# Which engine issues two kinds of DMA, and how many buffers hold a state-space unit's inputs

## The chip, the cores and the metric

The kernel runs on one core of a Trainium2 chip. A core has five engines that run side by side, each through its own instructions in order: TensorE (PE, matrix products; its weight loads are shown as PEld), VectorE (DVE), ScalarE (ACT), GpSimd (POOL) and SyncE (SP, which only issues DMAs). SP, ACT and POOL can issue DMAs; the bytes are carried by 16 DMA engines beside them. An instruction that waits for another engine or for a DMA waits in its place, and whatever stands behind it on the same engine waits with it.

The metric is the device time of one execution in microseconds; lower is better.

## The reference

One layer of a hybrid encoder, for one sequence of 2048 frames and 1024 channels, in float32. One normalised input `h` goes through one projection; its columns feed a diagonal state-space mixer (32 groups of 16 channels, 64 complex states each) and chunked attention (8 heads of 64, each chunk of 64 frames looks at itself and 8 chunks to its left). Both outputs are normalised, joined and projected, and a gated feed-forward network follows.

```python
h = rmsnorm(x, norm_mix_g[l])
proj = h @ w_in[l]
u_ssm, q, k, v = ...            # columns of proj
y_ssm = s5_mixer(u_ssm, ...)    # states = scan(lam_bar, B u); y = Re(C states) + D u; GELU, GLU
y_att = chunked_attention(q, k, v, attn_rel_bias[l])
mixed = concatenate([rmsnorm(y_ssm, ...), rmsnorm(y_att, ...)])
x = x + mixed @ w_out[l]
h2 = rmsnorm(x, norm_ffn_g[l])
x = x + (silu(h2 @ w_gate[l]) * (h2 @ w_up[l])) @ w_down[l]
return rmsnorm(x, norm_final_g)
```

## The kernel before

The work runs in stages: a prologue that builds the state-space matrices together with the projection of `u` (to about 150 us), the attention stage (about 150 to 720 us), the join and output projection (to about 1000 us), the gate and up products and then the down product. Matrix products are made from three float32r products of high and low halves (`mm3`, or the same three lines written out), which is why most operands exist as a "hi" and a "lo" tile.

The planner of the kernel's language places tiles in buffers, adds the waits, and orders the instructions of each engine: it keeps to the order of the code as a priority, and takes a later instruction first where an earlier one is not ready by its own estimate. TensorE's instructions are pinned to the order of the code (`Ordered`, `k.ta`, `k.te`); those of ACT, DVE, POOL and SP in the attention stage mostly are not.

**The attention stage** (`att_phase`) is a list of 128 steps: 4 blocks of 512 frames (`sb`), 4 pairs of heads (`pr`), 2 heads of a pair (`hh`), 4 groups of 128 queries (`qp`). A step issues, in this order, the scores of step s (`scores`: products `sc`, then on DVE the bias and the row extreme, line 846, then on ACT the exponential, line 849); the transposes of step s - 2 (`transp`: products `pt` into the only bank of that name, copied by ACT as `pth`, line 864, and by DVE as the low half `ptl`, line 865); the products with V (`pv_head`, `pv_scale`); and then parts of "units" that fill TensorE's time:

* `qk_unit(sb, pr)`: projects the queries (c = 0) and the keys (c = 1) of a pair of heads. The result of the queries lies in one bank `pf`, the first head in partitions 0 to 63, the second in 64 to 127. For each head, ACT writes the high half `q2h` into its own 64 partitions (line 769), DVE the low half `q2l` (line 770), and two DMAs, lines 771 and 772, copy each half into the other 64 partitions of the same tile. The second head's ACT instruction comes behind the first head's DVE instruction, since both read the one bank.
* `v_unit`, and `hT_unit`, which loads and normalises the next block's input (`xt`, `hi`, `lo`; lines 714 to 729).
* `ssm_unit(b)`, b = 0 to 7: four groups of 16 state-space channels each. It loads the frames `U` (8 DMAs), the input matrices `Bst`, the Toeplitz matrices `Tm` (8 DMAs) and the state-output matrices `Vm`, all issued by SP (line 567). After 8 empty turns the first product, `U` with `Bst`, goes through ACT (line 591) into the tile `X`. POOL scans `X` over time (lines 605 to 617) and copies the states with four DMAs to `XG` (line 639). After 9 more empty turns come the second products: `U` with `Tm` plus `XG` with `Vm`, copied by ACT (line 649) into `Y`, which shares its single buffer with `X`. Eight DMAs (line 652), issued by SP, store `Y` to memory as `S["y"]`. A unit fills 15 of the 128 steps, and the next follows.

`U`, `Bst`, `Tm` and `Vm` have one buffer each. The loads of the next unit's `U`, `Tm` and `Vm` can thus be issued only when the products of the unit before have read them. Unit 0's loads alone are pinned in the order of the code. In the units POOL is the engine `eng`.

The join (`mix_phase`) reads `S["y"]` back as `yr` (line 1030) in four loads for two blocks of frames, each load waiting for the stores of two units; GELU on ACT follows (line 1034), then the products of the gate (`gh`, `gl`).

POOL writes the descriptors of its own DMAs into a space of SBUF that the program reserves when it is made; its size was the default, 16384 bytes of each partition.

Of the kernel before, what the change touches and what calls it, by code (L numbers as in the profile page):

```python
# [16 lines left out]
P = 128  # L17
# [3 lines left out]
NG, CH, NS = 32, 16, 64  # L21
NPR = NG // 2
L = 8
NC = SEQ // L
GB, GP = 4, 2
# [81 lines left out]
def f32(ap):  # L107
    return ap.bitcast(F32)
# [48 lines left out]
def mm3(te, out, whi, wlo, xhi, xlo, first, last, **kw):  # L157
    te.matmul(out, whi, xhi, start=first, stop=False, **kw)
    te.matmul(out, whi, xlo, start=False, stop=False, **kw)
    te.matmul(out, wlo, xhi, start=False, stop=last, **kw)  # L160
# [399 lines left out]
def ssm_unit(k, p, psum, S, b, eng):  # L560

    nc = k.nc
    F = GB * CH
    U = k.t(p, "U", [P, GB, NC])

    def load(out, in_):
        ins = nc.sync.dma_start(out, in_)
        if b == 0:
            k.tc.keep_in_program_order(ins)

    for j in range(L):
        load(U[j * CH : (j + 1) * CH], S["u"][b * F : (b + 1) * F, j, :].rearrange("(g c) t -> c g t", c=CH))
    gs = slice(GB * b, GB * b + GB)
    bst = k.t(p, "Bst", [P, GB, P])
    load(bst[:].rearrange("p g m -> p (g m)"), S["bst"][b // 2][:, (b % 2) * GB * P : (b % 2 + 1) * GB * P])
    tm = k.t(p, "Tm", [P, GB, P])
    for i in range(L):
        load(tm[i * CH : (i + 1) * CH], S["kt"].rearrange("c g a m -> c g (a m)")[:, gs, P - CH * i : 2 * P - CH * i])
    vm = k.t(p, "Vm", [P, GB, P])
    load(vm[:], S["v"].rearrange("q g c n m -> (c n) (q g) m")[:, gs, CH:])  # L580
    for _ in range(YL):
        yield

    X = k.t(p, "X", [P, 2, GP, NC])
    for q in range(GP):
        ps = k.t(psum, "pj", [P, 2, NC], bufs=2)
        for g2 in range(2):
            k.ta.matmul(ps[:, g2, :], bst[:, 2 * q + g2, :], U[:, 2 * q + g2, :], start=True, stop=True)
        for g2 in range(2):
            for c in range(2):  # L590
                nc.scalar.copy(X[g2 * NS : (g2 + 1) * NS, c, q, :], ps[c * NS : (c + 1) * NS, g2, :])  # L591
        yield

    a8 = S["a8"]
    qs = slice(GP * b, GP * b + GP)
    Xk = X[:].rearrange("p r q (k s) -> p r q k s", s=8)
    Xe = Xk[:, :, :, :, 7].rearrange("p r q (a b) -> p r q a b", b=8)

    def step(dst, src, e, n):

        ar = a8[:, 0, qs, (0, 7, 15)[e]].unsqueeze(1).to_broadcast([P, 2, GP]).unsqueeze(3).to_broadcast([P, 2, GP, n])
        aw = S["sw"][:, e, :, qs].unsqueeze(3).to_broadcast([P, 2, GP, n])
        t = k.t(p, "st1", [P, 2, GP, NC // 8])
        t2 = k.t(p, "st2", [P, 2, GP, NC // 8])
        eng.tensor_tensor(t[:, :, :, :n], src, ar, op=ALU.mult)  # L605
        eng.tensor_tensor(t2[:, :, :, :n], src[:, ::-1], aw, op=ALU.mult)
        eng.tensor_tensor(dst, dst, t[:, :, :, :n], op=ALU.add)
        eng.tensor_tensor(dst, dst, t2[:, :, :, :n], op=ALU.add)

    def carry(dst, end, i0, n):  # L610

        for c in range(2):
            for e in range(2):
                t = k.t(p, "fx", [P, GP, NC // 8, 7])[:, :, :n]
                pw = a8[:, c if e == 0 else 1 - c, qs, i0 : i0 + 7].unsqueeze(2).to_broadcast([P, GP, n, 7])
                eng.tensor_tensor(t, end[:, e].unsqueeze(3).to_broadcast([P, GP, n, 7]), pw, op=ALU.mult)
                eng.tensor_tensor(dst[:, c], dst[:, c], t, op=ALU.subtract if e == 1 and c == 0 else ALU.add)
            yield

    for s in range(1, 8):  # L620
        step(Xk[:, :, :, :, s], Xk[:, :, :, :, s - 1], 0, NC // 8)
        yield
    for b_ in range(1, 8):
        step(Xe[:, :, :, :, b_], Xe[:, :, :, :, b_ - 1], 1, 4)
        yield
    for a in range(1, 4):
        step(Xe[:, :, :, a : a + 1, 7], Xe[:, :, :, a - 1 : a, 7], 2, 1)
        yield
    yield from carry(Xe[:, :, :, 1:, :7], Xe[:, :, :, :3, 7], 8, 3)
    yield from carry(Xk[:, :, :, 1:, :7], Xk[:, :, :, : NC // 8 - 1, 7], 0, NC // 8 - 1)  # L630

    if b == 0:
        k.XG = k.t(p, "XG", [P, GB, NC])
        nc.gpsimd.memset(k.XG[:, :, 0:1], 0.0)
    XG = k.XG
    XGv = XG[:].rearrange("p (q g) c -> p q g c", g=2)
    for g2 in range(2):
        for c in range(2):
            eng.dma_start(XGv[c * NS : (c + 1) * NS, :, g2, 1:], X[g2 * NS : (g2 + 1) * NS, c, :, : NC - 1])
    for _ in range(YX):  # L640
        yield
    Y = k.t(p, "X", [P, GB, NC])
    for q in range(GP):
        ps = k.t(psum, "pj", [P, 2, NC], bufs=2)
        for g2 in range(2):
            g = 2 * q + g2
            k.ta.matmul(ps[:, g2, :], tm[:, g, :], U[:, g, :], start=True, stop=False)
            k.ta.matmul(ps[:, g2, :], vm[:, g, :], XG[:, g, :], start=False, stop=True)
        nc.scalar.copy(Y[:, 2 * q : 2 * q + 2, :], ps[:])
        if q == GP - 1:  # L650
            for j in range(L):
                nc.sync.dma_start(S["y"][b * F : (b + 1) * F, j, :].rearrange("(g c) t -> c g t", c=CH), Y[j * CH : (j + 1) * CH])
        yield


# [25 lines left out]
def att_phase(k, ident, S):  # L681
    tc, nc, io = k.tc, k.nc, k.io
    with ExitStack() as cx:
# [16 lines left out]
        def keep_w(n):  # L700
            if n in keep:
                (k.Q if n in (0, 4) else nc.sync).dma_start(S["ws"][n], f32(keep.pop(n)[:]))
# [33 lines left out]
        def qk_unit(sb, pr):  # L736
            ws = [load_w(sb, n) for n in (pr, 4 + pr)]
            yield
            hi, lo = hT[sb]
            if (sb, pr) == (0, 0):  # L740
                ts = [[k.t(aw, f"{n}{q}x", [P, SB], F32R) for n, q in (("hi", hh), ("lo", hh), (("hi", "lo")[hh], 2))] for hh in range(2)]
            else:
                ts = [(k.t(aa, "q2h", [P, SB], F32R, bufs=3), k.t(aa, "q2l", [P, SB], F32R, bufs=3), k.t(aa, "k2", [P, 2 * SB], F32R, bufs=3)) for _ in range(2)]
            qk[sb, pr] = ts
            if sb > 0:
                for hh in range(2):
                    nc.sync.dma_start(f32(ts[hh][2][:, :SB]), S["k"][(sb - 1) % 2, 2 * pr + hh])
            both = (sb, pr) == (0, 0)
            pss = []
            for c in range(2):  # L750
                if c == 0 or not both:
                    cc = range(2) if both else (c,)
                    pss += [k.t(pfs, "pf", [P, 512]) for _ in cc]
                    for q in range(KT):
                        cs = slice(q * P, (q + 1) * P)
                        for m in cc:
                            wh, wl = ws[m]
                            mm3(k.ta, pss[m][:], wh[:, cs], wl[:, cs], hi[q][:], lo[q][:], q == 0, q == KT - 1)
                            if q == 2:
                                keep_w(4 * m + pr)  # L760
                        if q < KT - 1:
                            yield
                ps = pss[c]
                for hh in range(2):
                    q2h, q2l, k2 = ts[hh]
                    a = slice(hh * 64, hh * 64 + 64)
                    o = slice(64 - hh * 64, 128 - hh * 64)
                    if c == 0:
                        nc.scalar.activation(q2h[a, :], ps[a, :], AF.Copy, scale=-0.125)
                        nc.vector.scalar_tensor_tensor(q2l[a, :], ps[a, :], -0.125, f32(q2h[a, :]), op0=ALU.mult, op1=ALU.subtract)  # L770
                        nc.sync.dma_start(f32(q2h[o, :]), f32(q2h[a, :]))
                        nc.sync.dma_start(f32(q2l[o, :]), f32(q2l[a, :]))
                    else:
                        nc.scalar.copy(k2[a, -SB:], ps[a, :])
                        nc.vector.tensor_tensor(k2[o, -SB:], ps[a, :], f32(k2[a, -SB:]), op=ALU.subtract)
                        if sb < NSB - 1:
                            nc.sync.dma_start(S["k"][sb % 2, 2 * pr + hh], f32(k2[:, -SB:]))
                yield
# [926 lines left out]
```

## Time and profile before

| | |
|---|---|
| time, median of 3 runs | 2311.45 us (2308.72 to 2311.48) |
| the profiled execution: its own time | 2304.9 us |
| the profiled execution: span from the first to the last instruction | 2303.1 us |
| mean granted TensorE clock in it | 0.975 |
| DMA issues of U, in KB each | 64 of 64 KB, by SP |
| DMA issues of Tm and of Vm | 64 of 32 KB and 8 of 256 KB, by SP |
| DMA issues of y | 64 of 64 KB, by SP |
| moves of q2h and of q2l | 30 of 128 KB each, and 2 each of the first unit in other tiles, by SP |
| DMA issues of XG | 32 of 127.5 KB, by POOL |

The views used below are: the page's list of busy times; busy time by stretches of the span; the waits of an engine (who waited, `<-`, for whom: us in total, times, longest us); the timeline of one engine (start us, length us, instruction, count, and in brackets the idle time before it with what ended it); and the list of the instructions that touch one tile or come from one line, with the shortest, the median and the longest duration in ns. `L567` is line 567 of the kernel. A name such as `pj<-U,Bst` is a tile and what it is computed from. A DMA row gives the time of its issue on the engine that issues it; the landing is given apart. A busy time counts no DMA issue of SP or ACT and no wait.

### The profile page before, as it was taken

The numbers are of one execution on the slowest core, as the hardware profiler recorded it, in microseconds if no ns is written. First come the engines' busy times: TensorE is split into PE (matmuls) and PEld (weight loads), VectorE is DVE, ScalarE is ACT, GpSimd is POOL, SyncE is SP. The second block draws the span as 40 slices with busy tenths as digits, with TensorE's granted clock in tenths as the row PEclk, the third lists the DMA queues.
The fourth block names the chain that finished last, engine by engine and source line by source line (L and its number), as shares of the span: only waits on it lengthen the run. The fifth ranks groups of instructions, "written<-read, shape, count | busy, mean of one in ns | idle before, by whom it ended". The sixth has DMA issues, their size and how long they took to land.

```text
span 2303.1 us, 30454 instructions
## 1 busy us (share of the span) xinstructions
PE 2183.8 (95%) x10568; PEld 1834.1 (80%) x10568; DVE 1487.8 (65%) x2286; ACT 1001.3 (43%) x1675; POOL 1061.0 (46%) x1245
## 2 busy tenths in 40 slices
PE   8978799999997899989999999999999999999997
PEld 6667688898986788778888887888888878888886
DVE  7845555656555756676775669766645376578676
ACT  6335555555557542343333335333333343344332
POOL 3416655455660433265555554555555314445442
PEclk9989999999998999999999999999999999999998
DMA  8788766766653534754554556555433287465552
GB/s 295 260 286 265 235 210 204 207 190 193 192 137 114 178 118 163 249 165 143 167 193 157 205 190 254 195 193 167 158 96 110 76 326 265 165 228 183 201 182 74
DMA packets 216370, 437.00 MB, mean 190 GB/s; under 512 B 27352, under 2 KB 58120, under 8 KB 209112
## 3 DMA queue, kind: packets, MB, share of 16 engines
q1 hardware_dynamic: 211352, 420.89, 55.0%
q0 software_dynamic: 4864, 14.17, 1.9%
q8 instruction: 83, 1.36, 0.2%
q14 instruction: 71, 0.58, 0.1%
HBM read 294.98 MB, written 132.15 MB: 185 GB/s over the span
## 4 chain that ended last, share of the span: by engine, by line
PE 59%; DVE 3%; DMA 1%; ACT 1%; issue 1%; POOL 1%; SPq 0%; DVEq 0%; ACTq 0%; POOLq 0%
PE X L74 20%; PE ps L74 18%; PE Y L74 10%; PE big L74 6%; PE W L74 5%; DVE acc L1575 1%; DMA lo<-hc 0%; DMA x<-xt 0%; DVE xt L1117 0%; DVE lo L166 0%; DVE hd L166 0%; POOL c L166 0%; ACT hi L165 0%; POOL sa L1125 0%; DMA gl<-x 0%
## 5 line engine op out<-in xcount | busy, mean ns | idle before, releaser
L74 PE MATMUL X<-hi,c 128*128 128x512 f32 x1408 | 452.2, 392 | 7.6 <-ACT u L1391 3.5
L74 PE MATMUL ps<-hd,hd 128*128 128x512 f32 (+1 forms) x1968 | 431.7, 381 | 3.9 <-DVE hd L166 3.7
L74 PEld LDWEIGHTS ps<-hd,hd 128*128 128x128 f32 x1968 | 358.8, 190 | 75.5 <-DVE hd L166 5.1
L166 POOL TENSOR_TENSOR c<-S,c 128x512 fp32r<-128x512 f32 x176 | 253.1, 1440 | 260.7 <-ACT c L165 258.8
L74 PEld LDWEIGHTS X<-hi,c 128*128 128x128 f32 x1408 | 265.8, 189 | 65.2 <-ACT u L1391 5.1
L74 PE MATMUL X<-lo,c 128*128 128x512 f32 x704 | 275.3, 391 | 0.0
L166 POOL TENSOR_TENSOR hd<-hd 128x1536 fp32r<-128x1536 f32 (+1 forms) x46 | 159.1, 3463 | 232.0 <-ACT hd L165 218.8
L166 POOL TENSOR_TENSOR c<-raw,c 128x512 fp32r<-128x512 f32 x132 | 189.0, 1432 | 137.5 <-ACT c L165 109.1
L165 ACT CAST hd<-hd 128x1536 fp32r<-128x1536 f32 (+1 forms) x106 | 147.4, 1393 | 219.4 <-DMA hd<-hq 134.5
L74 PE MATMUL Y<-hi,c 128*128 128x512 f32 x704 | 225.5, 391 | 4.8 <-DVE u L1395 4.8
L1521 DVE TENSOR_TENSOR acc<-acc,ps 128x512 f32<-128x512 f32 x196 | 129.2, 681 | 79.5 <-PE ps L74 79.1
L74 PE MATMUL big<-m,woh 128*128 128x512 f32 x512 | 165.4, 404 | 0.6 <-DVE m L166 0.4
L165 ACT CAST c<-S 128x512 fp32r<-128x512 f32 x176 | 109.5, 622 | 116.5 <-PE Y L74 59.1
L74 PE MATMUL pf<-hi,w 128*128 128x512 f32 x416 | 150.9, 415 | 9.4 <-ACT hi L729 5.8
L74 PEld LDWEIGHTS Y<-hi,c 128*128 128x128 f32 x704 | 132.6, 188 | 33.9 <-DVE u L1395 6.3
L74 PEld LDWEIGHTS X<-lo,c 128*128 128x128 f32 x704 | 133.0, 189 | 27.7
L1391 ACT COPY u<-X 128x512 f32<-128x512 f32 x132 | 77.1, 585 | 177.5 <-PE X L74 177.5
L846 DVE CUSTOM_DVE_ANT_0 s<-sc,nb 128x640 f32<-128x640 f32 (+4 forms) x128 | 94.4, 737 | 89.4 <-PE sc L74 85.9
L605 POOL TENSOR_TENSOR st<-X,a 128x128 f32<-128x128 f32 (+2 forms) x136 | 47.4, 349 | 220.0 <-ACT X L591 157.4
L165 ACT CAST c<-raw 128x512 fp32r<-128x512 f32 x132 | 82.1, 622 | 143.1 <-PE Y L74 80.3
L166 DVE TENSOR_TENSOR hd<-hd 128x1536 fp32r<-128x1536 f32 (+1 forms) x60 | 119.3, 1990 | 31.2 <-ACT hd L165 30.5
L74 PE MATMUL Y<-lo,c 128*128 128x512 f32 x352 | 137.2, 390 | 0.0
(462 smaller groups left out, 4644.2 us busy)
## 6 DMA issues: line engine op xcount, KB each, us to landing
w<-wss SPq DMA_DIRECT2D x36, 1024.0 KB, 5.5
hq<-g SPq DMA_DIRECT2D x140, 256.0 KB, 2.1
hd<-hq SPq DMA_DIRECT2D x42, 768.0 KB, 4.5
hd<-wc SPq DMA_DIRECT2D x42, 768.0 KB, 6.0
raw<-in_w_gate SPq DMA_DIRECT2D x44, 512.0 KB, 3.7
raw<-in_w_up SPq DMA_DIRECT2D x44, 512.0 KB, 4.1
wc<-px SPq DMA_DIRECT2D x66, 256.0 KB, 3.2
wss<-w SPq DMA_DIRECT2D x12, 1024.0 KB, 5.6
```

Of the source, the lines that this page charges most:

```text
L74: return self.tc.keep_in_program_order(self.tc.nc.tensor.matmul(*a, **b))
L165: (hi_eng or nc.scalar).copy(hi, raw)
L166: (lo_eng or nc.gpsimd).tensor_tensor(lo, raw, f32(hi), op=ALU.subtract)
L605: eng.tensor_tensor(t[:, :, :, :n], src, ar, op=ALU.mult)
L846: nc.vector.tensor_tensor_reduce(s[:, :nk].rearrange("p (a b) -> p a b", a=nch), ps[:, :nch, :half], hd.nb[:, nk - 1 :: -1].rearrange("p ( ...
L1391: nc.scalar.copy(u[:], ps[:])
L1521: V.tensor_tensor(a, a, ps[:], op=ALU.add)
L1575: nc.vector.scalar_tensor_tensor(v, v, k.go[:, i : i + 1], self.rs[:, : self.n], op0=ALU.mult, op1=ALU.mult)
```

## The change

Five edits. The unit's `U`, `Tm` and `Vm` get two buffers each, which is 8 KB more of each partition. The eight stores of `Y` are issued by the unit's own engine, POOL. The moves of the query halves are issued by ACT. The reserved space for POOL's descriptors is halved to 8192 bytes.

```diff
@@ ssm_unit
-    U = k.t(p, "U", [P, GB, NC])
+    U = k.t(p, "U", [P, GB, NC], bufs=2)
...
-    tm = k.t(p, "Tm", [P, GB, P])
+    tm = k.t(p, "Tm", [P, GB, P], bufs=2)
...
-    vm = k.t(p, "Vm", [P, GB, P])
+    vm = k.t(p, "Vm", [P, GB, P], bufs=2)
...
             for j in range(L):
-                nc.sync.dma_start(S["y"][b * F : (b + 1) * F, j, :].rearrange("(g c) t -> c g t", c=CH), Y[j * CH : (j + 1) * CH])
+                eng.dma_start(S["y"][b * F : (b + 1) * F, j, :].rearrange("(g c) t -> c g t", c=CH), Y[j * CH : (j + 1) * CH])
@@ qk_unit
-                        nc.sync.dma_start(f32(q2h[o, :]), f32(q2h[a, :]))
-                        nc.sync.dma_start(f32(q2l[o, :]), f32(q2l[a, :]))
+                        nc.scalar.dma_start(f32(q2h[o, :]), f32(q2h[a, :]))
+                        nc.scalar.dma_start(f32(q2l[o, :]), f32(q2l[a, :]))
@@ kernel
-    nc = bacc.Bacc("TRN2", target_bir_lowering=False, num_devices=1)
+    nc = bacc.Bacc("TRN2", target_bir_lowering=False, num_devices=1, dynamic_dma_scratch_size=8192)
```

`Bst` and the tile `X` of `X` and `Y` keep one buffer. No arithmetic changes.

## The prediction, made before the changed kernel was run

> **What bounds the kernel now.** I began with the page: its span, and the busy time of each engine.
>
> ```profile
> span 2303.1 us, 30454 instructions
> PE 2183.8 (95%) x10568; PEld 1834.1 (80%) x10568; DVE 1487.8 (65%) x2286; ACT 1001.3 (43%) x1675; POOL 1061.0 (46%) x1245
> ```
>
> TensorE is busy 95% of the span, so an edit is worth what it takes from, or adds to, TensorE's idle time. All edited lines run in the attention stage. The view by stretches (us, then busy time of PE, PEld, DVE, ACT and POOL with instruction counts, granted clock, DMA share, GB/s) shows how tight that stage is:
>
> ```profile
> 175.00:700.00 525.00, 487.57 (x2954) 434.89 (x2952) 303.51 (x573) 291.20 (x614) 292.69 (x704) 0.98 0.68 205
> 550.00:600.00 50.00, 50.00 (x327) 46.24 (x326) 27.42 (x50) 27.89 (x56) 19.14 (x49) 1.00 0.63 184
> 600.00:650.00 50.00, 47.28 (x271) 42.17 (x270) 25.02 (x44) 27.12 (x54) 19.90 (x49) 0.97 0.61 172
> ```
>
> TensorE idles 37 us of these 525. DVE, ACT and POOL are busy a little over half: there is room on them, but it lies in pieces. What TensorE waits for there, in the view of waits of three stretches (150 to 240, 240 to 400, 560 to 690 us; total, times, longest):
>
> ```profile
> PE pj L74 <- DMA Tm<-kts: 1.1, 1, 1.1
> ```
> ```profile
> PE pf L74 <- ACT hi L729: 5.8, 2, 3.5
> PE pj L74 <- DMA U<-u: 1.6, 1, 1.6
> PE pj L74 <- DMA Tm<-kts: 0.6, 1, 0.6
> ```
> ```profile
> PE pj L74 <- DMA U<-u: 2.7, 1, 2.7
> ```
>
> Four state-space units (of 0 to 7) start late because their loads are late: 1.1 + 1.6 + 0.6 + 2.7 = 6.0 us. The two named Tm stand before the first product (U with Bst), which reads no Tm; I read them as the frames U too. Why the loads are late is read from SyncE's timeline around unit 7, and TensorE's beside it (start, length, instruction, idle time before it and its releaser):
>
> ```profile
> 630.28 0.32 SPq L567 DMA_DIRECT2D U<-u  x1
> ```
> ```profile
> 633.40 3.86 SPq L652 DMA_DIRECT2D y<-X  x8
> ```
> ```profile
> 637.77 3.27 SPq L567 DMA_DIRECT2D U<-u  x7
> ```
> ```profile
> 642.88 2.70 PE L74 MATMUL pj<-U,Bst 128*128 128x256 f32 x8 [2.72 <-DMA U<-u]
> ```
>
> The first frame load can be issued only when unit 6 has freed U; then come unit 6's eight stores, and only then the seven other loads. The engines that carry the bytes are not the cause: the order on SyncE and the single buffer are.
>
> **The change, part by part.** *Second buffers.* With two U, unit 7's frames need no longer wait for unit 6. Will their issue move ahead? The planner does move a load that is free: Bst of unit 2 was issued 29 us before the same unit's first frames, though both stand together in the code.
>
> ```profile
> 263.08 0.38 SPq L567 DMA_DIRECT2D Bst<-bsts  x1
> ```
> ```profile
> 292.14 0.33 SPq L567 DMA_DIRECT2D U<-u  x1
> ```
>
> The longest wait is 2.7 us; 29 us ahead removes it, so I take all of the 6.0 us. The bounds are 0 and 6.0. In the stretch 600 to 650, which holds the 2.7 us wait, the clock is 0.97 against 1.00 in the one before: 0.03 x 50 = 1.5 us, which I add (bounds 0 and 1.5). What is late next is the transposes (below).
>
> *Moves of queries on ACT.* Thirty and thirty moves leave SyncE's queue for ACT's:
>
> ```profile
> L771 SPq DMA_DIRECT2D q2h<-q2h x30: 461/467/605, 171.2 to 676.7; - x30
> L772 SPq DMA_DIRECT2D q2l<-q2l x30: 461/467/1404, 172.0 to 677.6; - x30
> ```
> ```profile
> SPq L771 <- ACT q2h L769: 29.1, 14, 6.1
> SPq L772 <- DVE q2l L770: 7.6, 23, 1.1
> ```
>
> On SyncE this takes 60 x 0.467 = 28 us and 36.7 us of waiting ahead of other loads; nothing but the frames above has TensorE waiting there, so the relief itself is priced at 0. On ACT, which issues no DMA before, an issue is bounded by SyncE's 0.461 and by 1.29 us (the first unit, below); I take 0.467, the same transfer. The q2h move needs only ACT's own result. The q2l move adds a real wait: it needs DVE's low part, on average 7.6/23 = 0.33 us after the q2h issue, and behind it in ACT's order stand exponentials and the copies of the transposes, on which TensorE soon waits. A unit has two halves. ACT already idles between them:
>
> ```profile
> ACT q2h L769 <- DVE q2l L770: 6.8, 9, 0.8
> ```
>
> That idle (6.8/9 = 0.76 us) holds the first issue. In strict order the others push ACT by 0.47 + 0.47 + 0.33 + 0.47 = 1.74 us. If the planner puts other work into the waits, about one issue (0.47) stays. Does it reach TensorE? The last tight place, in the timelines of ACT, DVE and PE, and the first one on PE:
>
> ```profile
> 633.11 0.69 ACT L864 CAST pth<-pt 128x640 fp32r<-128x640 f32 x1
> ```
> ```profile
> 633.84 0.82 DVE L865 TENSOR_TENSOR ptl<-pt,pth 128x640 fp32r<-128x640 f32 x1 [0.26 <-ACT pth L864]
> ```
> ```profile
> 634.74 0.63 PE L77 MATMUL pt<-ident,s 128*128 128x128 f32 x4
> ```
> ```profile
> 204.00 0.87 PE L77 MATMUL pt<-ident,s 128*128 128x128 f32 x3 [1.81 <-DVE ptl L865]
> ```
>
> There is one transpose bank. ACT copies it, DVE ends at 634.66, and TensorE refills it 0.08 us later: a later ACT is a later TensorE. I count five of the fifteen units with under 0.2 us of room behind the moves (near 204, 275, 345, 490 and 635); in the others the next transposes come 0.7 us or more after DVE. So 5 x 0.47 = +2.3 us. The bounds are 0 (all absorbed) and 5 x 1.74 = 8.7.
>
> The four moves of the very first unit also go to ACT, just ahead of the Toeplitz and projection copies:
>
> ```profile
> 128.73 1.29 SPq L772 DMA_DIRECT2D lo0x<-lo0x  x1
> ```
> ```profile
> 127.39 3.92 ACT L413 COPY kt<-pp 16x512 f32<-16x512 f32 x8
> ...
> 140.88 0.92 ACT L304 COPY bst<-pp 128x256 f32<-128x256 f32 x3 [3.87 <-DMA bsts<-bst]
> ```
>
> ACT there feeds POOL's bsts stores, whose landing ACT awaits at 140.88, so a push goes through. Two of four issues fit idle places; the other two cost between 0 and 2 x 1.29 = 2.6; I take 2 x 0.5 = +1.0.
>
> *Stores of y by POOL.* 64 issues, bounded by SyncE's (3.86/8 = 0.48) and POOL's own moves of XG:
>
> ```profile
> L639 POOL DMA_DIRECT2D XG<-X x32: 587/621/666, 212.3 to 685.4; - x32
> ...
> DMA to landing us min/median/max: 2.3/4.7/8.7
> ```
> ```profile
> DMA to landing us min/median/max: 2.0/2.2/3.9
> ```
>
> (The second landing row is of the present y stores.) I take 0.621: 5.0 us for a unit's eight, 40 us in all. Their cover is POOL's idle time between units: the stores wait for ACT's last copy of Y, and POOL's next work is the next scan, which needs ACT's new X. At the unit change I quote from ACT:
>
> ```profile
> 359.52 0.59 ACT L649 COPY X<-pj 128x512 f32<-128x512 f32 x1 [1.10 <-PE pj L74]
> ```
> ```profile
> 370.44 1.90 ACT L591 COPY X<-pj 64x256 f32<-64x256 f32 x5 [2.15 <-issue]
> ```
>
> From 360.11 to 370.44 are 10.3 us; 5.0 are used, so 0 on the path. Y and the next X share one buffer, though: without that cover the new X waits (a rival). Only the last unit's stores have a reader at once, the read-back yr:
>
> ```profile
> 695.27 3.63 SPq L652 DMA_DIRECT2D y<-X  x8
> 702.19 0.34 SPq L899 DMA_DIRECT2D ya_s<-ya  x1
> 702.77 0.53 SPq L1030 DMA_DIRECT2D yr<-y  x1
> ```
> ```profile
> 708.88 3.64 ACT L1034 ACTIVATE ys<-yr 128x2048 f32<-128x2048 f32 x1
> ```
> ```profile
> 713.61 0.79 PE L74 MATMUL pf<-gh,wgh 128*128 128x512 f32 x1 [6.76 <-ACT gh L165]
> ```
> ```profile
> yr<-y SPq DMA_DIRECT2D x8, 512.0 KB, 5.5
> ```
>
> From 695.3, POOL issues until 700.3, landing at 702.5 to 705.0. Today yr is issued at 702.77 behind another store and lands about 5.5 later, at 708.3, 0.6 before GELU begins. From the middle, 703.7, it lands at 709.2: +0.3 us (bounds 0 and 1.6).
>
> *The smaller descriptor space.* The smaller space for POOL's DMAs pays for the buffers. No row shows POOL waiting for it; I take 0.
>
> **Sum.** -6.0 - 1.5 + 2.3 + 1.0 + 0.3 = -3.9 us. The profiled execution took 2304.9 (its span and 1.8 around it), 6.6 under the median of 2311.45; I apply the difference to the median: **2307.5 us**.
>
> **The rivals.** (a) *More comes early.* SyncE, rid of waits, also issues the next block's input tiles sooner, and the 5.8 us wait on hi goes: -9.7, 2301.7. Against it: those tiles stand behind stores of k, which stay. (b) *ACT takes the gain.* Strict order: -7.5 + 8.7 + 2.2 + 0.3 = +3.7, 2315.2. For it: the single transpose bank; against it: a planner that fills waits. (c) *The change doesn't do what it says.* The loads stay late behind other waits on SyncE, and only costs are left: +3.6, 2315.1. The Trainium skill's "DMA: Bandwidth & Descriptors", section "Issuing engines are not separate DMA queues", says all issuers share the same 16 DMA engines and another issuer saves only issue time, usually small: by it (c) is the outcome. The order of unit 7's rows speaks against it. (d) *Slower: the stores hold X.* POOL's last store of a unit is issued 5.0 us after Y; if it lands over 4.7 us later (the median of POOL's XG, so this is the deciding point), the new X, ACT behind it, the scan and its product move. At 8.7, XG's maximum, it is 4.0 us at a unit change; for half of seven changes +14, together +10, 2321.6. For it: the shared buffer; against: stores to memory land in 2.2 us now. The Trainium skill's "SBUF - State Buffer", section "SBUF: two separate sides", warns that a DVE operation holding the shared port starves POOL's descriptor writing; POOL's 587 to 666 ns for 32 issues beside a busy DVE show none of it.
>
> **How the numbers follow.** About 0.2% (4.6 us) is what a measurement of this kernel can tell from no change, so faster is under 2306.8, slower over 2316.1. Forecast case 0.46 (its own range 2303 to 2311: 0.28 faster, 0.18 same); (a) 0.13 faster; (b) 0.17 (0.13 same, 0.04 slower); (c) 0.09 (0.06 same, 0.03 slower); (d) 0.15 (0.01 same, 0.14 slower). Sums: 0.41, 0.38, 0.21. The range 2300 to 2320 takes in (a), (b), (c) and the lighter half of (d).
>
> **What would show it.** Frames issued well before their unit's product and no TensorE wait on U or Tm: the first term. Clock 1.00 at 600 to 650: the second. Move issues on ACT near 0.47 us, and TensorE's wait on DVE ptl grown by 2 to 3 us: the third; by 8: (b). Eight stores on POOL in 5 us, the X copies not waiting on them: if they do, (d). I am wrong if the planner reorders ACT or DVE elsewhere in the stage, or the stall before 141 us changes by several us.

## The result, and the profile after

The changed kernel takes **2342.09 us** (median of 5 runs, 2337.61 to 2345.67) against 2311.48 for the kernel before in the same runs: 30.6 us more, a ratio of 1.0127 with a 95% interval from 1.0109 to 1.0144. The forecast was 2307.5, its range ended at 2320.

The page of the changed kernel begins:

```profile
span 2340.1 us, 30413 instructions
PE 2194.6 (94%) x10568; PEld 1838.8 (79%) x10568; DVE 1493.4 (64%) x2286; ACT 1002.6 (43%) x1675; POOL 1088.4 (47%) x1309
```

TensorE runs the same 10568 products in the same order, so the two traces can be laid side by side product by product. Up to 124 us they agree within 1 us. By the 500th product (about 138 us) the new one is 9.1 us behind, at the 1500th 15.0, at the 2000th 28.3, at the 3500th (704.6 us) 34.4; after that it gains and loses 1 to 2 us and ends 37.0 behind. Nearly all was lost before the end of the attention stage. (The two profiled executions lie 37.0 us apart, the medians 30.6; so what is read from these two traces adds up to some 6 us more than the change in the median.) The view by stretches for the same 3200 products, from the first `pp<-vg,bbg` on, before and after (length, busy PE, PEld, DVE, ACT, POOL, clock, DMA share, GB/s):

```profile
124.28:702.10 577.82, 527.00 (x3204) 470.16 (x3202) 324.49 (x617) 315.22 (x674) 297.10 (x713) 0.97 0.69 212
```
```profile
125.14:737.70 612.56, 538.47 (x3203) 476.92 (x3201) 323.92 (x617) 316.52 (x674) 329.61 (x777) 0.95 0.66 201
```

The stretch has grown by 34.7 us. TensorE idles 23.3 us more (74.1 against 50.8), and is busy 11.5 us longer with the same products, at a clock of 0.95 for 0.97. DVE and ACT have no more work than before: it is a matter of what waits for what. POOL's 32 us more are the 64 stores.

What was hoped for came. TensorE waits for no frame any more; unit 7's frames are all issued 70 us ahead of their product (timelines of SP and PE):

```profile
595.16 2.04 SPq L567 DMA_DIRECT2D U<-u  x4
601.68 1.87 SPq L567 DMA_DIRECT2D U<-u  x4
```
```profile
673.73 1.89 PE L74 MATMUL pj<-U,Bst 128*128 128x256 f32 x8
```

In the side-by-side view the first products of units 1, 2, 3 and 7 gain 1.30, 1.76, 0.80 and 2.88 us. What was paid stands in other waits (waits of TensorE, 140 to 740 us, before and after):

```profile
PE pt L77 <- DVE ptl L865: 13.5, 10, 2.6
...
PE pj L74 <- ACT X L591: 0.2, 1, 0.2
PE pj L74 <- DVE ptl L865: 0.2, 1, 0.2
```
```profile
PE pt L77 <- DVE ptl L865: 23.2, 12, 3.0
...
PE pj L74 <- DVE ptl L865: 7.4, 9, 1.4
PE pj L74 <- ACT X L591: 6.8, 2, 3.5
```

The waits for the low half `ptl` grew by 16.9 us, and those for the copies `X` of a unit's first product by 6.6. Two timelines of the changed kernel show one place of each kind. At 451 us DVE stands for a tile `xt`, and the copy `ptl` stands behind it, so TensorE waits for the transpose bank (2.40 us):

```profile
450.40 0.75 DVE L728 SCALAR_TENSOR_TENSOR xt<-xt,g_mix,rsn 128x512 f32<-128x512 f32 x1 [4.78 <-DMA xt<-in_xt]
451.07 0.82 DVE L865 TENSOR_TENSOR ptl<-pt,pth 128x640 fp32r<-128x640 f32 x1
```
```profile
451.94 0.77 PE L77 MATMUL pt<-ident,s 128*128 128x128 f32 x5 [2.40 <-DVE ptl L865]
```

That DVE waits for `xt` is only one of the ways in which `ptl` comes late: over the stage DVE waits no longer for `xt` than before (10.3 us against 10.8). At most of the other places a bias step (line 846) or the low half of another tile stands in front of `ptl`.

At 391 us ACT stands 3.61 us for an exponential whose row extreme is not there. The eight copies of unit 3's first product, which ended at 389.69, stand behind it:

```profile
391.24 0.83 ACT L849 ACTIVATE s<-s,mn 128x640 f32<-128x640 f32 x1 [3.61 <-DVE mn L846]
391.97 0.19 ACT L849 ACTIVATION_READ_ACCUMULATOR s<-s,mn 128x1 f32 x1
392.06 3.01 ACT L591 COPY X<-pj 64x256 f32<-64x256 f32 x8
```

In the kernel before the copies of this unit began at 370.44, ahead of that exponential (the prediction quotes the row). The order in which the planner put DVE's and ACT's instructions is different, although no arithmetic is.

### The profile page after: what moved, and what is told of

The parts are those of the page before. It is cut to its first block, busy times and chain, and to the rows that moved or that the text cites. A ratio compares the mean times of both kernels' runs of the same rounds, so it can differ in the third digit from the quotient of the medians.

```text
span 2340.1 us, 30413 instructions
## 1 busy us (share of the span) xinstructions
PE 2194.6 (94%) x10568; PEld 1838.8 (79%) x10568; DVE 1493.4 (64%) x2286; ACT 1002.6 (43%) x1675; POOL 1088.4 (47%) x1309
## 4 chain that ended last, share of the span: by engine, by line
PE 57%; DVE 4%; DMA 2%; issue 1%; ACT 1%; POOL 0%; SPq 0%; DVEq 0%; ACTq 0%; POOLq 0%
PE X L74 19%; PE ps L74 18%; PE Y L74 10%; PE big L74 5%; PE W L74 5%; DMA lo<-hc 1%; DVE lo L166 1%; DVE acc L1575 1%; DMA x<-xt 0%; DVE xt L1117 0%; DVE hd L166 0%; POOL sa L1125 0%; DVE u L1395 0%; DVE m L166 0%; DMA hd<-hq 0%
## 5 line engine op out<-in xcount | busy, mean ns | idle before, releaser
L166 DVE TENSOR_TENSOR hd<-hd 128x1536 fp32r<-128x1536 f32 (+1 forms) x60 | 124.5, 2076 | 32.6 <-ACT hd L165 32.3
L865 DVE TENSOR_TENSOR ptl<-pt,pth 128x640 fp32r<-128x640 f32 (+3 forms) x152 | 98.3, 647 | 50.7 <-ACT pth L864 49.3
```

Of the source, the lines that this page charges most:

```text
L166: (lo_eng or nc.gpsimd).tensor_tensor(lo, raw, f32(hi), op=ALU.subtract)
L865: nc.vector.tensor_tensor(ptl[:, a:b, qp, :], pt[:, a:b, :], f32(pth[:, a:b, qp, :]), op=ALU.subtract)
```

## The experiments

Each kernel is compared with the kernel before in runs on the same chip.

| kernel | median us | before us | ratio, 95% interval |
|---|---|---|---|
| the change | 2342.09 | 2311.48 | 1.0127 (1.0109 to 1.0144) |
| moves_only | 2341.38 | 2309.98 | 1.0136 (1.0116 to 1.0156) |
| first_moves_only | 2318.03 | 2309.98 | 1.0031 (1.0012 to 1.0049) |
| bufs_stores | 2317.08 | 2309.98 | 1.0029 (1.0019 to 1.0039) |
| bufs_only | 2321.33 | 2309.98 | 1.0047 (1.0031 to 1.0063) |
| change_first_on_SP | 2333.82 | 2307.87 | 1.0114 (1.0099 to 1.0129) |
| moves_held | 2319.67 | 2307.87 | 1.0047 (1.0030 to 1.0064) |
| change_held | 2323.03 | 2307.87 | 1.0053 (1.0036 to 1.0071) |
| bufs_stores_held | 2328.28 | 2307.87 | 1.0084 (1.0067 to 1.0101) |
| bufs_stores_held_SP | 2305.51 | 2307.87 | 0.9985 (0.9971 to 0.9999) |
| stores_held_SP | 2305.00 | 2307.87 | 0.9981 (0.9968 to 0.9995) |
| moves_but_first_held_SP | 2309.29 | 2307.87 | 1.0004 (0.9990 to 1.0018) |
| scratch_only | 2307.14 | 2307.87 | 0.9999 (0.9986 to 1.0012) |

**The parts by themselves.** moves_only is the kernel before with this edit alone:

```diff
-                        nc.sync.dma_start(f32(q2h[o, :]), f32(q2h[a, :]))
-                        nc.sync.dma_start(f32(q2l[o, :]), f32(q2l[a, :]))
+                        nc.scalar.dma_start(f32(q2h[o, :]), f32(q2h[a, :]))
+                        nc.scalar.dma_start(f32(q2l[o, :]), f32(q2l[a, :]))
```

> The kernel before with the third part alone: the 64 moves are issued by ACT. Theory A (the moves cost all): the whole loss and no gain on the frames, 2342 + 6 = about 2348, within 2340 and 2355. Theory B (early loads alter the order, moves cost in the prologue alone): 2311.5 + 9 = about 2320.

It costs 31.4 us, as much as the whole change. Theory A had 2348 for it, by adding back the 6 us of the frames; they are not to be had that simply, as the next two show. bufs_stores is the change with the moves back on SP, bufs_only has the second buffers and the smaller descriptor space alone.

```diff
# bufs_stores: the change, but
-                        nc.scalar.dma_start(f32(q2h[o, :]), f32(q2h[a, :]))
-                        nc.scalar.dma_start(f32(q2l[o, :]), f32(q2l[a, :]))
+                        nc.sync.dma_start(f32(q2h[o, :]), f32(q2h[a, :]))
+                        nc.sync.dma_start(f32(q2l[o, :]), f32(q2l[a, :]))
# bufs_only: besides this
-                eng.dma_start(S["y"][b * F : (b + 1) * F, j, :].rearrange("(g c) t -> c g t", c=CH), Y[j * CH : (j + 1) * CH])
+                nc.sync.dma_start(S["y"][b * F : (b + 1) * F, j, :].rearrange("(g c) t -> c g t", c=CH), Y[j * CH : (j + 1) * CH])
```

> The change without its third part: second buffers, stores of y on POOL and the smaller descriptor space stay, the 64 moves of query halves go back to SP. Theory A, the moves on ACT cost all that was lost: the first units' frames still come early (-6.0), the prologue's delay of about 9 us goes, and the stage loses nothing: 2311.5 - 6 = about 2305, within 2302 and 2309. Theory B, early loads alter the order on ACT and DVE and the moves only cost in the prologue: 2342 - 9 = about 2333. Theory C, the stores on POOL hold the shared buffer: also near 2333, with X copies of ACT that wait for landings of y.

> The second buffers with the smaller descriptor space that makes room for them; stores and moves on SP. Theory A: the frames still stand behind the stores of y and the moves in the queue of SP, so a part of the 6.0 us at most comes: 2306 to 2312. Theory B: about 2333 as for bufs_stores. If this is 2305 and bufs_stores too, the stores on POOL bring nothing.

Both are slower than the kernel before, by 7.1 and 11.4 us, and neither theory had that: A expected 2305 and at most 2312, B 2333. The runs of bufs_only lie far apart (2311 to 2330), and its profiled run is the lowest of them, so its trace isn't read for the loss, and what bufs_only lost stays open. In bufs_stores the frames gain the same 1.30, 1.76, 0.80 and 2.88 us, and the copies of `X` stand behind an exponential again:

```profile
377.79 0.83 ACT L849 ACTIVATE s<-s,mn 128x640 f32<-128x640 f32 x1 [2.73 <-DVE mn L846]
378.52 0.19 ACT L849 ACTIVATION_READ_ACCUMULATOR s<-s,mn 128x1 f32 x1
378.61 3.01 ACT L591 COPY X<-pj 64x256 f32<-64x256 f32 x8
```
```profile
PE pj L74 <- ACT X L591: 8.0, 2, 4.6
```

(The second row is of the waits of TensorE, 140 to 740 us; the kernel before has 0.2 there.) POOL's stores are not in this chain. In the changed kernel itself unit 2's stores are issued in 4.05 us, the last one is issued 8.3 us before the copies that begin at 392.06, and no store takes more than 5.1 us to land:

```profile
379.73 4.05 POOL L652 DMA_DIRECT2D y<-X  x8 [13.89 <-ACT X L649]
```

**The first unit's moves.** Two experiments on the same four instructions: only they on ACT, and all but they on ACT.

```diff
# first_moves_only: the kernel before, with
+                        ((nc.scalar if (sb, pr) == (0, 0) else nc.sync)).dma_start(f32(q2h[o, :]), f32(q2h[a, :]))
+                        ((nc.scalar if (sb, pr) == (0, 0) else nc.sync)).dma_start(f32(q2l[o, :]), f32(q2l[a, :]))
# change_first_on_SP: the change, with nc.sync and nc.scalar the other way round
```

> The kernel before with only the four moves of the very first unit on ACT. If the delay of about 9 us before 138 us comes from these four (loads of SP that reuse a completion semaphore of an ACT move wait for that move's landing, so vg is issued 6.8 us later), this takes 2311.5 + 9 = about 2320, with vg again issued some 6 us later than in the kernel before. If it is only the issue time on ACT (4 x 0.5 us and the waits on them), as the prediction had it: 2312 to 2314. If the delay comes from the changed order of other loads: 2311.

> The whole change, but the four moves of the first unit stay on SP. If the loads vg wait for the landings of these moves on ACT: vg is issued near 120 us again, TensorE has no wait on vg, and the time is 2342 - 7 = about 2335, within 2330 and 2339. If the prologue's loss comes from elsewhere: 2342.

Four DMA issues cost 8.0 us (2.8 to 11.3 by the interval), with the planner's own order of everything else. In the waits of SP (118 to 135 us; the changed kernel) the loads of `vg`, the state-output matrices of the prologue, wait for landings of moves with which they share no tile:

```profile
SPq L403 <- DMA hi0x<-hi0x: 5.4, 1, 5.4
SPq L403 <- DMA lo0x<-lo0x: 3.9, 1, 3.9
```

The trace's semaphores say why. Each DMA of SP or ACT signals one of the same eight completion semaphores (101 to 108), handed out in turn in the planner's order, and is issued only when the DMA that had the semaphore before has landed (in the changed kernel's trace all 887 issues whose predecessor's landing is known come after it):

```
                vg issued   semaphore awaited   who had it (issue, landing)
before          119.39      105                 an earlier DMA of SP, landed
                120.30      106                 an earlier DMA of SP, landed
                122.06      107                 an earlier DMA of SP, landed
the change      126.19      101                 hi0x move on ACT (123.92, 126.12)
                130.62      102                 lo0x move on ACT (126.28, 130.54)
                131.47      103                 hi1x move on ACT (127.66, 131.39)
```

By these numbers the planner expected the four moves early: three of them stand eight places ahead of a load of `vg` each. On SP the issue order is one for both; on ACT the moves wait for their projection until 123.9 and after, and SP's loads wait with them. TensorE stands twice (its timeline in the changed kernel):

```profile
123.81 1.92 PE L74 MATMUL pp<-vg,bbg 128*16 128x128 f32 x16
130.82 3.35 PE L74 MATMUL pp<-vg,bbg 128*16 128x128 f32 x16 [5.10 <-DMA vg<-vs]
135.61 3.67 PE L74 MATMUL pp<-vg,bbg 128*16 128x128 f32 x32 [1.44 <-DMA vg<-vs]
```

In change_first_on_SP `vg` is issued at 119.43 again and the delay at the 500th product is 0.1 us in place of 9.1, as expected. Of this the time shows only a part: the ratio falls from 1.0127 to 1.0114, about 3 us, with intervals that overlap. At the 4000th product the profiled run is 28.1 us behind the kernel before, the change's 33.9: of the 9 us saved at the 500th product some 6 are left, and the rest went into later waits.

**The order held.** 31.4 us for moves_only less 8.0 leaves 23 us. Is it ACT, held up by issuing (A1), or the planner's other order (A2)? The following kernels carry a list of the DVE and ACT instructions (DMAs left out) in the order in which they stand in the kernel before, and bind each to the one ahead of it, in issue order alone:

```diff
     with tile.TileContext(nc) as tc:
         block_kernel(tc, io)
+        hold(tc)
...
+def hold(tc):
+    ins = {i.name: i for i in tc.nc.cur_bb.bb.instructions}
+    for text in HELD:
+        names = [n for n in ("I-" + t for t in text.split()) if n in ins]
+        for a, b in zip(names, names[1:]):
+            tc.add_manual_dep(ins[b], a, mybir.DependencyInfo(mybir.DependencyClass.NoSync, mybir.DependencyReason.DATA), reason="held")
```

> All 64 moves on ACT as in moves_only (2341), but the order of every other instruction of ACT and of DVE is held as in the kernel before, by edges that only fix the issue order; the moves themselves may stand anywhere between them. Theory A1, ACT is held up by issuing the moves and by their waits: the loss stays, 2336 to 2346. Theory A2, the planner, which no longer sees the moves in SP's queue, places multiplications of xt and other waiting work of DVE and ACT earlier than the loads come, and the transposes' copies stand behind them: only the loss before 141 us is left, 2310 + 7 = about 2317, within 2312 and 2322.

moves_held takes 11.8 us over the kernel before in place of 31.4, within the range of A2. Some 20 us of the moves' price were the order. If the first four moves take 8.0 of the 11.8, as they do by themselves, the other 60 issues cost about 3.8. The waits show the difference (140 to 740 us; DVE's for `xt`, and TensorE's for the low half of the transposes, in moves_only and then in moves_held):

```profile
DVE xt L728 <- DMA xt<-in_xt: 19.0, 10, 6.6
...
PE pt L77 <- DVE ptl L865: 20.5, 9, 3.8
...
PE pj L74 <- DVE ptl L865: 8.7, 7, 3.4
```
```profile
DVE xt L728 <- DMA xt<-in_xt: 10.5, 7, 3.3
...
PE pt L77 <- DVE ptl L865: 14.4, 13, 2.9
...
PE pj L74 <- DVE ptl L865: 0.3, 2, 0.2
```

With its queue free of moves, SP was planned to load `xt` sooner (in moves_only two loads are issued at 205.72 and 206.25, which stand at 215.62 and 216.10 in the kernel before), and DVE's work on it was put ahead of copies `ptl`. On the chip the load still came late. This fits the trace of moves_only; which of the two, SP's freedom or ACT's new burden, made the planner move the rest was not tried apart.

> The whole change (2342) with the order of ACT and DVE held as in the kernel before. Theory A2: loss before 141 us and gain on the frames, 2310 + 7 - 6 = about 2311, within 2306 and 2317. Theory A1: 2310 + 31 - 6 = about 2335.

> Second buffers, stores of y on POOL and the smaller descriptor space, moves on SP, as in bufs_stores (2317), with the order of ACT and DVE held as in the kernel before. Theory A2 (the changed order eats the gain of the early frames): 2310 - 6 = about 2304, within 2300 and 2307, and no X copy of ACT that stands behind an exponential which itself waits. If the early loads themselves cost (transfers in the way of others): about 2317 as before.

change_held came at a ratio of 1.0053 instead of 1.0127: about 17 us of the change's loss were the order, and 15.2 us are left where A2 expected about 1. bufs_stores_held failed altogether: expected 2304, measured 2328, worse by 11 us than with the planner's own order. Both misses have one cause, seen in SP's timeline of bufs_stores_held and DVE's beside it:

```profile
215.12 4.55 SPq L567 DMA_DIRECT2D U<-u  x7
222.29 0.34 SPq L567 DMA_DIRECT2D Bst<-bsts  x1
222.67 5.48 SPq L567 DMA_DIRECT2D Tm<-kts  x8
228.19 0.43 SPq L567 DMA_DIRECT2D Vm<-vs  x1
...
229.69 1.75 SPq L714 DMA_DIRECT2D xt<-in_xt  x2
```
```profile
235.89 0.75 DVE L728 SCALAR_TENSOR_TENSOR xt<-xt,g_mix,rsn 128x512 f32<-128x512 f32 x1 [13.62 <-DMA xt<-in_xt]
236.56 0.42 DVE L865 TENSOR_TENSOR ptl<-pt,pth 128x256 fp32r<-128x256 f32 x1
```
```profile
237.12 1.09 PE L77 MATMUL pt<-ident,s 128*128 128x128 f32 x4 [5.89 <-DVE ptl L865]
```

In the kernel before these loads of `xt` stood ahead of the unit's frames:

```profile
215.62 0.93 SPq L714 DMA_DIRECT2D xt<-in_xt  x2
```

Seventeen loads, all but `Bst` into a second buffer, have gone ahead of them and fill SP's queue from 215.12 to 228.62. DVE's old order does not know of it: it waits 13.62 us, `ptl` behind it, and TensorE with both. In all DVE waits 36.5 us for `xt` (10.8 in the kernel before). In change_held the unit's loads stand ahead of the same two loads of `xt` too, which are issued at 237.48; DVE waits 11.35 us there, and 24.0 in all.

**SP's order held too.** The last group shows whether that is all. In the first two SP's list is added to those of DVE and ACT, with nothing gone from it but the stores; the third also has the later units' moves on ACT (SP's list leaves out what another engine issues); the fourth is the descriptor space alone.

```diff
# bufs_stores_held_SP: bufs_stores, with HELD for DVE, ACT and SP
# stores_held_SP: the kernel before, with the same lists and
-                nc.sync.dma_start(S["y"][b * F : (b + 1) * F, j, :].rearrange("(g c) t -> c g t", c=CH), Y[j * CH : (j + 1) * CH])
+                eng.dma_start(S["y"][b * F : (b + 1) * F, j, :].rearrange("(g c) t -> c g t", c=CH), Y[j * CH : (j + 1) * CH])
# moves_but_first_held_SP: change_first_on_SP, with the same lists
# scratch_only: the kernel before, with
+    nc = bacc.Bacc("TRN2", target_bir_lowering=False, num_devices=1, dynamic_dma_scratch_size=8192)
```

> As bufs_stores_held (2328), but SP's order too is held as in the kernel before; only the stores of y have gone from it to POOL. The unit's frames keep their place behind the loads of xt, and are issued without the eight stores ahead of them and without waiting for the unit before. Theory A3, in bufs_stores_held the 17 or so early loads of a unit stand ahead of the loads of xt, and DVE with the copies of the transposes behind xt: that goes, DVE waits some 11 us for xt as in the kernel before, the frames' waits go too: 2308 - 6 = about 2302, within 2298 and 2306. If POOL's stores or the second buffers cost by themselves: 2312 or more.

> The stores of y on POOL alone, one buffer each, default descriptor space, order of ACT, DVE and SP held. The frames of units 2, 3 and 7 are issued without the eight stores ahead but still wait for the unit before. If the order on SP made them late: 2308 - 3 to 5 = 2303 to 2305. If the single buffer did: 2308. If POOL's stores hold the shared X: above 2312.

> As bufs_stores_held_SP, with the 60 moves of the later units on ACT and the first unit's four on SP. What it takes over bufs_stores_held_SP is the price of the issues on ACT by themselves, with no change of order: by the prediction's term 2.3 us (bounds 0 and 8.7); by moves_held less the loss before 141 us, 11.8 - 7 = about 5.

> The smaller descriptor space alone. The prediction had 0. As the tiles move in SBUF and the planner's order of DVE, ACT and SP changes in a few lines, -3 to +3 us; beyond this a part of what bufs_stores lost belongs to it.

bufs_stores_held_SP, with the very parts of bufs_stores_held, is 22.8 us faster than it and now ahead of the kernel before, by 2.4 us (0.2 to 6.7 by the interval). DVE's wait for `xt` falls to 14.9 us, somewhat over the 10.8 of the kernel before (bufs_stores_held, then bufs_stores_held_SP):

```profile
DVE xt L728 <- DMA xt<-in_xt: 36.5, 12, 13.6
```
```profile
DVE xt L728 <- DMA xt<-in_xt: 14.9, 12, 3.5
```

stores_held_SP, without any second buffer, does as well (2.9 us). So with the orders held neither the buffers nor POOL's stores show a cost, and the stores alone bring what is to be had. The rest of the frames' 6 us stays out because frames that keep their place on SP are still late: in the two profiled runs unit 7's first product waits 0.86 and 1.14 us, where it waited 2.72, and unit 2's waits 2.04 and 1.89, where it waited 1.60. Both kernels are faster than the kernel before, barely.

moves_but_first_held_SP is 3.8 us over bufs_stores_held_SP, so the 60 issues cost a few us here too. Their intervals overlap a little, and that moves_held gave 3.8 as well is chance: each of the two figures can be off by several us. scratch_only is 0.7 us under the kernel before, with 1 inside the interval.

One pair answers for the change itself. change_first_on_SP and moves_but_first_held_SP have the same edits and differ only in the orders of DVE, ACT and SP: the planner's new ones (ratio 1.0114), or those of the kernel before (1.0004). That is some 25 us for the orders, and with them held the edits, but for the first four moves, cost nothing that is clear of noise.

## Why the prediction was wrong

The step that failed is the one on the moves: it priced issues and waits within the old order of ACT's and DVE's work, and had no term for another order. Another order took most of what was lost. By its own steps:

* *Second buffers, -6.0.* Right as a forecast of the wait: 6.7 us came in the four places named. Wrong as a term of the sum. The step read "What is late next is the transposes" and priced them under the moves alone. What the 17 loads of a unit overtake on SP was not asked, though the prediction had asked it the other way round in rival (a), "SyncE, rid of waits, also issues the next block's input tiles sooner". In bufs_stores_held two of those tiles were issued 14.1 us later instead, and DVE stood 13.6 us for them.
* *The clock, -1.5.* It did not come. From 600 to 650 us the changed kernel shows 1.00, but other products run then: the products that filled this stretch before run from 631.9 to 684.5 us, at 0.97 again. The price of new waits in clock was not counted either; products ran 11.5 us longer in the stage.
* *Moves on ACT, +2.3 with bounds 0 and 8.7.* For the issues themselves the size was right: 468 ns each in the median, and about 3.8 us for all, give or take a few. What failed is the sentence "If the planner puts other work into the waits, about one issue (0.47) stays". It took the planner for something that only fills gaps. In moves_only it set DVE and ACT to another order throughout the stage, for some 20 us. The upper bound was that of a strict order in the old sequence, and so no bound: by the prediction's own sign TensorE's wait for `ptl` was to grow by 2 to 3 us, or by 8 under (b), and it grew by 16.9.
* *The first unit's moves, +1.0 with bounds 0 and 2.6.* The term was mis-sized: 8.0 us measured. It was argued as a push on ACT; the price was paid on SP, where `vg` waited for the moves' landings.
* *Stores on POOL, +0.3.* Right, near enough: each store is issued in 512 ns, not 621, a unit's eight in 4.05 us; the join's first product waits 7.47 us where it waited 6.76, and 6.8 again in stores_held_SP. This row of the changed kernel stands against that of the prediction:

```profile
L652 POOL DMA_DIRECT2D y<-X x64: 512/512/524, 237.8 to 735.2; - x64
...
DMA to landing us min/median/max: 2.2/3.0/5.1
```

* *The descriptor space, 0.* Right (scratch_only).

Of the rivals, (a) did not come: the wait on `hi` is 4.3 us in place of 5.8. (b) named the right edit and a mechanism that is worth 3.8 us. (c) fell: the frames came 70 us early. (d) fell too: no new `X` waited for a store; in the changed kernel every unit's stores had landed 4.7 us or more before the next unit's copies. The Trainium skill's "SBUF — State Buffer", section "SBUF: two separate sides", warns that a DVE operation that holds the shared port keeps POOL from writing descriptors, which would have spoken for (d). Here the 64 stores were issued in 512 to 524 ns each beside a DVE that was busy 64% of the span, and show no sign of it. Two slips of the prediction's arithmetic decided nothing: (b) takes 2.2 for the first unit's moves without saying from what, and (d) sets 4.7 us as the deciding landing where its own 10.3 less 5.0 leaves 5.3. The prediction closed with "I am wrong if the planner reorders ACT or DVE elsewhere in the stage, or the stall before 141 us changes by several us". Both happened, and together they are nearly all of it. Of the 31.4 us for the moves alone, about 8.0 come from the first four moves, about 3.8 from the other issues and about 20 from the order. Of the 30.6 us for the whole change, the orders of DVE, ACT and SP are some 25, and the first four moves the rest, 3 by the ratios and 5 by the medians; all else comes to 1.4, not clear of noise. With the orders of DVE and ACT alone held, 15.2 us remain (change_held), and this can't be split by adding up terms: bufs_stores_held, with no move on ACT, loses 20.4 under the same held orders. Which of the planner's many new places cost how much was not measured one by one.

## What to carry to other kernels

Where a planner orders some engines, an edit that moves an issue from one queue to another is an edit of every order that the planner derives; hold the orders of the kernel before to see what the edit itself costs, and only then ask what a new order brings. A load that is freed from a buffer goes ahead of something: look for what stood behind it in the same queue and who waits for that. DMAs of two engines can be tied by shared completions, so a move that is issued late on one engine can hold loads of the other that have nothing to do with it.

## What the runs showed of the hardware

The slower clock after a wait was not expected at this size. In the changed kernel TensorE waited 3.33 us for the `X` copies above, and for 6 us after it the granted clock was half (its timeline, and stretches: length, PE busy, clock, DMA share, GB/s):

```profile
393.60 0.80 PE L74 MATMUL pj<-pth,v 128*128 128x512 f32 x1 [3.33 <-ACT X L591]
```
```profile
394.00:396.00 2.00, 2.00 (x8) 0.50 0.40 81
396.00:398.00 2.00, 2.00 (x7) 0.50 0.02 2
398.00:400.00 2.00, 2.00 (x12) 0.50 0.00 0
400.00:402.00 2.00, 2.00 (x18) 0.99 0.00 0
```

Laid beside the kernel before, TensorE loses 6.1 us from just before this wait to 402 us, half of it in the wait and half in the products behind it. In the stage a third of the loss (11.5 of 34.7 us) is products that ran longer.

Not every wait has this. After one of 2.98 us the clock stayed at 1.00; after a shorter one, of 2.83 us, it was lower, at 0.60 and 0.55 in stretches of 2 us:

```profile
227.81 0.52 PE L77 MATMUL pt<-ident,s 128*128 128x128 f32 x3 [2.98 <-DVE ptl L865]
...
444.69 1.30 PE L77 MATMUL pt<-ident,s 128*128 128x128 f32 x5 [2.83 <-DVE ptl L865]
```
```profile
228.00:230.00 2.00, 2.00 (x19) 1.00 1.12 146
```
```profile
444.00:446.00 2.00, 1.31 (x6) 0.60 1.05 296
446.00:448.00 2.00, 2.00 (x6) 0.55 0.85 235
```

The Trainium skill's "TensorE: Matmul & The Clock Gate", section "What's actually happening", says that the clock is halved after an idle window of about 3.4 us, and that this window runs freely. The trace agrees with the length and with the free running, and these show why the two waits differ. Its clock records change only at multiples of 3.41 us from one another: half from 393.20 to 400.03 and from 444.40 to 447.82. Of the wait of 2.83 us, 2.54 lie in the one step that ends at 444.40; the wait of 2.98 us is cut by the grid at 225.95 into 1.12 and 1.86. But a step need not be idle throughout. From 100 to 748 us of the changed kernel, every step at full clock with 1.95 us or more of idle TensorE was followed by half clock, and all but one (1.32 us) of those with 1.88 us or less by full clock. TensorE's idle time is taken from the trace, where the ends of its products are modelled.
